# A decoder layer on one core: mixing buffers, four MLP down steps, and the final norm laid out differently

## The chip, the core and the metric

One NeuronCore of a Trainium2 chip runs the whole layer. Its engines are TensorE (PE in the profile: matmuls; PEld is its weight load), VectorE (DVE), ScalarE (ACT), GpSimd (POOL) and SyncE (SP), which issues the DMAs in order. Data live in SBUF (128 partitions), products are summed in PSUM (eight banks of 128x512 float32). The metric is the device time of one execution in microseconds; less is better. TensorE's clock has two levels, 1.2 and 2.4 GHz; the profile shows the granted clock as a fraction of the upper one.

## The reference, cut to what matters

With 1024 tokens and a model width of 1024 the layer computes

```python
u = rms_norm(x, norm_mix_g);  proj = u @ w_in
attn  = dilated_attention(rope(q), rope(k), v)       # 8 heads of 64, three window patterns
mlstm = sigmoid(mo) * rms(mlstm_chunkwise(q, k, v, gates))   # 4 heads of 128
h = x + concat(attn, mlstm) @ w_out
h = h + relu(rms_norm(h, norm_mlp_g) @ w_up) ** 2 @ w_down   # inner width 4096
h = h + sigmoid(rms_norm(h, norm_ple_g) @ w_ple_gate) * (p @ w_ple)
out = rms_norm(h, final_norm_g)
```

in float32. A reduced precision is not close enough, so every operand of a large product is split into a high and a low float32r part, and a product is three matmuls.

## The kernel before

All activations are held transposed: channels on partitions, tokens along the row, in KT = 8 blocks k of 128 channels and NCH = 2 halves c of CH = 512 tokens. `split` makes the two parts of an operand: a cast on ScalarE (L92) for the high part, a subtraction on VectorE (L93) for the low one. `mm3` issues wh·xh, wh·xl and wl·xh (L101 to L103).

**Order.** The program is written stage by stage, and a scheduler with planned costs of its own puts each engine's instructions, and SyncE's DMAs, into one fixed order, in which an engine works whatever the true times are. A tile of a pool waits until the tile that lay on its bytes before is no longer read; where one pool follows another this holds tile by tile.

**Mixing.** The projections and four pairs of attention heads work in a pool mp; when it is closed, the four mLSTM heads work in pools sp and cp on the same bytes. Attention results go to DRAM (mixd, L435), the values to vd (L446), mLSTM results to mixmd (L648). `head(h)` loads q and k as r, then qw (L547), the values vr (L567), and the decay weights w (L590). TensorE's transposes kt give kw, and `upd` (L576) updates the state with vr and kw. Beside the heads run the projections mvp of later heads. `load_pair` (L538) loads the mixed results `in` again and splits them into mixa (attention) and mixm (mLSTM), the operands of the out projection. `in` shares the tag "stage", four buffers, with other short-lived tiles, the t of the first out projection among them.

**First out projection.** `out_first(k)` sums four of the eight contributions: for each k and half, a tile t is loaded from xT (L663), the product o of twelve matmuls is added to it (L664), and it is stored to hd (L665). The rest of the out projection comes later.

**MLP.** MLP up runs 16 blocks f, each a scheme of seven products in place of eight. Its results zz and zt are stored to DRAM (zd, L891 and L898). MLP down has seven products D_OPS of eight steps g; a step is 24 matmuls d. For each step y (from zd) and wd are loaded raw, in a pool rawp, and split in a pool of two pairs (hl2) or in one of a single pair (hl1), in turn: every third step takes hl1. These pools lie on the bytes of the pools of MLP up: rawp and hl2 on the first ones, hl1 on the last, zu1, which holds the last block's result until it is stored. Only the first two steps are split into pairs of the general pool that MLP up has freed (`first`). After them come the additions to h (L1083).

**Gated embedding and final norm.** Four blocks o of 256 channels: seven products pg each (`embed`), the last block in two pieces of 256 tokens of each half. `gate` makes h of a channel block and token range: multiplication, tanh, two more on VectorE (L1133 to L1136), then h squared on ScalarE (L1140) and the running sum of squares fin, printed as state (L1144). `final_cols` sums the squares over channels with 128x1 matmuls cs (L1173), makes ra (L1178, VectorE) and rb, the reciprocal root (L1179, GpSimd). `final` spreads rb to rows with transposes bp (L130), copies them (L1187), and multiplies each of eight channel blocks by gain and row: on VectorE in one step (L1193), or on ScalarE and GpSimd (L1195, L1196). outT is stored channels first (L1199), and transposed on the host.

## Time and profile before

| | us |
|---|---|
| median of 3 runs | 1385.82 (1381.39 to 1387.63) |
| the profiled execution | 1385.74 |
| its span | 1383.9 |
| TensorE busy | 1330.2 (96%) |
| VectorE busy | 1021.7 (74%) |
| ScalarE busy | 655.6 (47%) |
| GpSimd busy | 58.0 (4%) |
| mean granted clock of TensorE | 0.982 |

All times in the trace count from the span's start. MLP down starts at 964.5, and the last product of the embedding ends at 1365.8. A row of a timeline with a count groups like instructions that follow each other; the name after the arrow is what is read.

### The profile page before, as it was taken

The page shows a single profiled execution, that of the slowest core. Times are in us where ns is not written, and L with a number is a line of the kernel's source. Part 1 is how long each engine was busy: PE and PEld are TensorE (multiplying, and loading weights), DVE is VectorE, ACT ScalarE, POOL GpSimd, SP SyncE. Part 2 cuts the span into 40 slices and gives each one's busy share as a digit, 9 for nine tenths or more (in the row PEclk, how much of TensorE's full clock was granted, in tenths as well). Part 3 has the DMA queues.
Part 4 walks back from the last instruction along what each step waited for, and adds up shares of the span by engine and source line. Part 5 has one row for each costly group of instructions (what it writes and reads, how often), then busy time and mean ns, then how long its engine had stood idle before and what let it go on. Part 6 is the DMA issues. An engine that isn't in the chain of part 4 may idle for free. (4 is left out here: it accounts for less than half of the span.)

```text
span 1383.9 us, 18363 instructions
## 1 busy us (share of the span) xinstructions
PE 1330.2 (96%) x6795; PEld 1120.7 (81%) x6795; DVE 1021.7 (74%) x1774; ACT 655.6 (47%) x1039; POOL 58.0 (4%) x55
## 2 busy tenths in 40 slices
PE   8999999999979998899999999999899999999995
PEld 6988888988859887788887888888788888888884
DVE  7797579599758885599666676667457875778895
ACT  7465545644446442258443334435234333565553
POOL 1100000000000000000000000000000210001002
PEclk9999999999999999999999999999999999999997
DMA  6111012123226347555154344446879773671323
GB/s 233 48 50 35 24 52 68 59 78 97 76 60 209 119 167 243 172 183 212 55 219 151 154 169 166 156 155 256 282 223 333 295 272 111 208 248 62 107 91 122
DMA packets 79018, 208.26 MB, mean 150 GB/s; under 512 B 7536, under 2 KB 19728, under 8 KB 74320
## 3 DMA queue, kind: packets, MB, share of 16 engines
q1 hardware_dynamic: 78928, 207.09, 43.6%
q8 instruction: 53, 0.87, 0.3%
q14 instruction: 37, 0.30, 0.1%
HBM read 146.74 MB, written 60.32 MB: 150 GB/s over the span
## 5 line engine op out<-in xcount | busy, mean ns | idle before, releaser
L102 PE MATMUL u<-x,wuh 128*128 128x512 f32 x448 | 177.0, 395 | 0.0
L101 PE MATMUL u<-x,wuh 128*128 128x512 f32 x448 | 174.7, 395 | 0.0
L103 PE MATMUL u<-x,wul 128*128 128x512 f32 x448 | 171.9, 395 | 1.0 <-DVE wul L93 1.0
L101 PE MATMUL d<-yh,wdh 128*128 128x512 f32 x432 | 166.0, 393 | 4.1 <-ACT wdh L92 3.7
L102 PE MATMUL d<-yl,wdh 128*128 128x512 f32 x432 | 168.7, 392 | 0.0
L103 PE MATMUL d<-yh,wdl 128*128 128x512 f32 x432 | 168.1, 391 | 0.0
L93 DVE TENSOR_TENSOR wul<-wu_r,wuh 128x768 fp32r<-128x768 f32 (+1 forms) x64 | 69.6, 1087 | 65.2 <-ACT wuh L92 65.2
L103 PEld LDWEIGHTS u<-x,wul 128*128 128x128 f32 x448 | 84.3, 188 | 21.1 <-DVE wul L93 1.4
L102 PEld LDWEIGHTS u<-x,wuh 128*128 128x128 f32 x448 | 84.4, 188 | 20.1 <-DVE x L93 0.4
L101 PEld LDWEIGHTS u<-x,wuh 128*128 128x128 f32 x448 | 84.3, 188 | 19.7
L101 PEld LDWEIGHTS d<-yh,wdh 128*128 128x128 f32 x432 | 81.7, 190 | 21.9 <-ACT wdh L92 4.2
L102 PEld LDWEIGHTS d<-yl,wdh 128*128 128x128 f32 x432 | 81.8, 189 | 17.2
L103 PEld LDWEIGHTS d<-yh,wdl 128*128 128x128 f32 x432 | 81.5, 189 | 16.9
L909 ACT COPY tmp<-u 128x512 f32<-128x512 f32 x48 | 28.1, 588 | 109.1 <-PE u L103 109.0
L92 ACT CAST wuh<-wu_r 128x768 fp32r<-128x768 f32 (+1 forms) x64 | 59.1, 943 | 43.2 <-PE u L102 22.2
L92 ACT CAST wdh<-wd_r 128x1024 fp32r<-128x1024 f32 x30 | 31.6, 1053 | 81.1 <-PE d L102 77.7
L93 DVE TENSOR_TENSOR wdl<-wd_r,wdh 128x1024 fp32r<-128x1024 f32 x30 | 36.6, 1220 | 43.8 <-ACT wdh L92 43.8
L410 ACT ACTIVATE pr<-pr,mn 128x128 f32<-128x128 f32 (+3 forms) x64 | 49.5, 774 | 41.0 <-PE av L413 23.4
L93 DVE TENSOR_TENSOR yl<-y_r,yh 128x1024 fp32r<-128x1024 f32 x54 | 65.6, 1216 | 0.0
L405 DVE CUSTOM_DVE_ANT_0 pr<-s,biasS 128x512 f32<-128x512 f32 (+2 forms) x96 | 51.0, 551 | 12.3 <-PE tp L420 7.2
L92 ACT CAST yh<-y_r 128x1024 fp32r<-128x1024 f32 x54 | 56.5, 1047 | 7.1 <-DMA y_r<-zd 7.1
L93 DVE TENSOR_TENSOR pl<-tp,ph 128x512 fp32r<-128x512 f32 (+1 forms) x80 | 49.7, 631 | 10.7 <-ACT ph L92 6.3
(393 smaller groups left out, 3410.4 us busy)
## 6 DMA issues: line engine op xcount, KB each, us to landing
wd_r<-wdown SPq DMA_DIRECT2D x72, 512.0 KB
y_r<-zd SPq DMA_DIRECT2D x56, 512.0 KB
wu_r<-wup SPq DMA_DIRECT2D x32, 512.0 KB
zd<-zz SPq DMA_DIRECT2D x16, 1024.0 KB
zd<-zt SPq DMA_DIRECT2D x16, 1024.0 KB
wm_r<-wmqk SPq DMA_DIRECT2D x8, 512.0 KB
wo_r<-wout SPq DMA_DIRECT2D x16, 256.0 KB
hs<-h SPq DMA_DIRECT2D x8, 512.0 KB
```

The lines of the kernel that those rows point to most:

```text
L92: S.copy(hi, src)
L93: V.tensor_tensor(lo, src, hi.bitcast(F32), op=ALU.subtract)
L101: PE.matmul(ps, wh, xh, start=start, stop=False, skip_group_check=more)
L102: PE.matmul(ps, wh, xl, start=False, stop=False, skip_group_check=more)
L103: PE.matmul(ps, wl, xh, start=False, stop=stop, skip_group_check=more)
L405: V.tensor_tensor_reduce(pr[:, ks], s[:, :n], biasS[:, b0 + o:b0 + o + n], 1.0, -2 * LOW, op0=ALU.add, op1=ALU.min, accum_out=mn[:, o // C ...
L410: S.activation(pr[:, :nk], pr[:, :nk], AF.Exp, scale=-1.0, bias=mn[:, :1], accum_out=den)
L909: S.copy(tmp[key], ps)
```

## The change

It has three parts.

*Mixing.* cosS and sinS are allocated ahead of KL in mp, which moves other tiles of that pool. In `head`, vr is loaded, and its ones are set, first, ahead of r and qw. `load_pair` gets four buffers of its own for `in`, in cp.

*MLP down.* Two more pairs for y and two for wd (`ahead`) are taken from the general pool before MLP up is closed, so the first four steps of product b11 lie there. The pairs for sw are taken when they are first written.

*Final norm.* h of a block and range is multiplied by its gain on ScalarE once its square is taken. The squares of k = 6 and k = 7 stay apart from fin, so that a column sum has three sources. The 64 blocks of 128x128 of h are transposed by TensorE (`turned`) into fixed PSUM banks, so that tokens lie on partitions, and rb becomes a factor for each partition: `result` multiplies 128x512 at a time from PSUM on ScalarE or VectorE, and stores outN, tokens first. No rows are spread, and the host transposes nothing.

```diff
+    cosS = mp.tile([P, T], F32, name="cosS", bufs=1)
+    sinS = mp.tile([P, T], F32, name="sinS", bufs=1)
     KL = [[mp.tile([P, T], F32R, name=f"kl{i}{a}", bufs=1) for a in range(2)] for i in range(2)]
...
     S.mul(ghalf, col[:, C_MG:C_MG + MH], 0.5)
-    cosS = mp.tile([P, T], F32, name="cosS", bufs=1)
-    sinS = mp.tile([P, T], F32, name="sinS", bufs=1)
     biasS = mp.tile([P, T], F32, name="biasS", bufs=1)
...
             sl = slice(c * CH, (c + 1) * CH)
-            r = stage("in")[:, :CH]
+            r = cp.tile([P, CH], F32, name="in", bufs=4)
             nc.sync.dma_start(r, src[:, sl])
...
     def head(h, qk=(None, None)):
+        vr = cp.tile([P, NB, P + 1], F32, name="vr", bufs=1)
+        nc.sync.dma_start(vr[:, :, :P], vd[h // 2, :, :, (h % 2) * P:(h % 2 + 1) * P])
+        V.memset(vr[:, :, P:], 1.0)
         r = raw(qkd[h]) if qk[0] is None else qk[0]
...
         vv = (unit("mv"), unit("mv"))
-        vr = cp.tile([P, NB, P + 1], F32, name="vr", bufs=1)
-        nc.sync.dma_start(vr[:, :, :P], vd[h // 2, :, :, (h % 2) * P:(h % 2 + 1) * P])
-        V.memset(vr[:, :, P:], 1.0)
         split([v.rearrange("p (b c) -> p b c", c=P) for v in vv], vr[:, :, :P])
...
                 if fresh:
-                    bank[b] = acc_tile(name)[:, :width]
+                    bank[b] = (banks[b] if banks else acc_tile(name))[:, :width]
                 for i in range(n):
...
         first = [[split(pair(n), r) for n, r in zip(("y", "wd"), raws)] for raws in first]
+        ahead = [[pair(n) for n in ("y", "wd")] for _ in range(2)]
         up_scope.close()
...
         def parts(name, tag, src):
+            if ahead and tag == "y":
+                return split(ahead[0][0], src)
+            if ahead:
+                return split(ahead.pop(0)[1], src)
             pool = hl1 if made[tag] % 3 == 2 else hl2
...
         A11, A12, A21, A22 = range(4)
-        sp4 = [pair("s", F32) for _ in range(NG // 2)]
-        sw = [sp4[g // 2][g % 2] for g in range(NG)]
+        sw = []
         def weights(key, g):
...
                 a, b = wraw(g, A21), wraw(g, A22)
+                if g % 2 == 0:
+                    sw.extend(pair("s", F32))
                 V.tensor_tensor(sw[g], a, b, op=ALU.subtract)
...
                 S.activation(fin[:, sl], h[k][:, sl], AF.Square)
+                S.mul(h[k][:, sl], h[k][:, sl], col[:, C_GFIN:C_GFIN + 1])
                 return
             S.activation(ga, h[k][:, sl], AF.Square)
-            if k == KT - 1:
-                last[sl.start] = ga
+            if k >= KT - 2:
+                last[k, sl.start] = ga
             else:
                 V.tensor_tensor(fin[:, sl], fin[:, sl], ga, op=ALU.add)
-        def embed(o, off=0, n=CH, hooks={}):
+            S.mul(h[k][:, sl], h[k][:, sl], col[:, C_GFIN + k:C_GFIN + k + 1])
+        def embed(o, off=0, n=CH, hooks={}, banks=None):
             tmp = {}
...
                     f()
-            products(wblocks[o], X, ev, "pg", off=off, width=n)
+            products(wblocks[o], X, ev, "pg", off=off, width=n, banks=banks)
+        FINAL = [slice(c * CH + a, c * CH + a + L) for a in (0, L) for c in (1, 0)]
         cols_of = {}
-        def final_cols(i):
+        def sums(i, *which):
             sl = FINAL[i]
-            nt = (sl.stop - sl.start) // P
-            cs = acc_tile("cs3")
-            for j in range(nt):
-                for src in (fin[:, sl], last[sl.start]):
-                    PE.matmul(cs[:, j:j + 1], src[:, j * P:(j + 1) * P], ones, start=src is not last[sl.start],
-                              stop=src is last[sl.start])
-            a = zp.tile([P, nt], F32, name="ra3", tag="ra")
-            b = cols_of[i] = zp.tile([P, nt], F32, name="rb3", tag="rb")
-            at = slice(sl.start // P, sl.stop // P)
-            V.scalar_tensor_tensor(a, cs[:, :nt], 1.0 / D, seps[:, at], op0=ALU.mult, op1=ALU.add)
-            G.tensor_tensor(b, a, mhalf[:, :nt], op=ALU.pow)
-        def final(i):
-            sl = FINAL[i]
-            n = sl.stop - sl.start
-            bp = acc_tile("bp3")
-            bcast_rows(bp, cols_of[i], n // P)
-            rows = small("rows")[:, :n]
-            S.copy(rows, bp[:, :n])
-            outs = wcp.tile([P, 8, L], F32, name="out", tag="wc")
-            for k in range(KT):
-                o = outs[:, k]
-                gain = col[:, C_GFIN + k:C_GFIN + k + 1]
-                if k in ON_V[i]:
-                    V.scalar_tensor_tensor(o, h[k][:, sl], gain, bp[:, :n], op0=ALU.mult, op1=ALU.mult)
-                else:
-                    S.mul(o, h[k][:, sl], gain)
-                    G.tensor_tensor(o, o, rows, op=ALU.mult)
-                if k + 1 in TO[i]:
-                    k0 = max(t for t in (0,) + TO[i] if t <= k)
-                    nc.sync.dma_start(outT[k0:k + 1, :, sl].rearrange("k p t -> p k t"), outs[:, k0:k + 1])
-        ON_V = ((0, 1, 3, 4, 6), (0, 1, 3, 4, 6, 7), (0, 1, 3, 4, 6), (0, 2, 3, 5, 6, 7))
-        TO = ((4, 8), (4, 8), (4, 8), (2, 4, 6, 8))
-        FINAL = [slice(c * CH + a, c * CH + a + L) for a in (0, L) for c in (1, 0)]
+            n = L // P
+            to = [banks[3 if i == 3 and j else 0][:, CH // 2 + 2 * i + j:CH // 2 + 2 * i + j + 1] for j in range(n)]
+            for j, src in ([(j, src) for src in which for j in range(n)] if i == 3 else
+                           [(j, src) for j in range(n) for src in which]):
+                at = fin[:, sl] if src == "fin" else last[src, sl.start]
+                PE.matmul(to[j], at[:, j * P:(j + 1) * P], ones, start=src == "fin", stop=src == KT - 1)
+            if KT - 1 in which:
+                a = zp.tile([P, n], F32, name="ra3", tag="ra")
+                b = cols_of[i] = zp.tile([P, n], F32, name="rb3", tag="rb")
+                t0 = sl.start // P
+                for at in ((slice(0, 1), slice(1, 2)) if i == 3 else (slice(0, 2),)):
+                    src = banks[3 if at.start else 0][:, CH // 2 + 2 * i + at.start:CH // 2 + 2 * i + at.stop]
+                    V.scalar_tensor_tensor(a[:, at], src, 1.0 / D, seps[:, t0 + at.start:t0 + at.stop],
+                                           op0=ALU.mult, op1=ALU.add)
+                G.tensor_tensor(b, a, mhalf[:, :n], op=ALU.pow)
+        def turned(i, ks, js=(0, 1)):
+            for k in ks:
+                for j in js:
+                    t0 = FINAL[i].start + j * P
+                    PE.transpose(banks[TB[i][2 * j + k // 4]][:, k % 4 * P:(k % 4 + 1) * P], h[k][:, t0:t0 + P], ident)
+        def result(i):
+            outs = wcp.tile([P, 8, L], F32, name="out", tag="wc").rearrange("p a b -> p (a b)")
+            tb = FINAL[i].start // P
+            for j in range(2):
+                for q in range(2):
+                    o = outs[:, j * D + q * CH:j * D + (q + 1) * CH]
+                    src = banks[TB[i][2 * j + q]]
+                    r = cols_of[i][:, j:j + 1]
+                    if (q if i >= 2 else 2 * j + q == 1):
+                        V.tensor_scalar(o, src, r, None, op0=ALU.mult)
+                    else:
+                        S.activation(o, src, AF.Copy, scale=r)
+                    nc.sync.dma_start(outN[tb + j, :, q * CH:(q + 1) * CH], o)
+        TB = ((2, 5, 6, 7), (2, 5, 6, 7), (1, 4, 5, 2), (6, 7, 1, 4))
         fetch(0)
...
         fetch_emb(NO - 1)
-        embed(NO - 1, 0, L)
-        embed(NO - 1, L, L, hooks={"b11": [lambda: final_cols(0)], "b22": [lambda: final(0)],
-                                   "t3": [lambda: final_cols(1)], "t4": [lambda: final_cols(2)]})
-        final_cols(3)
-        for i in range(1, 4):
-            final(i)
+        banks = [acc_tile("fin") for _ in range(8)]
+        embed(NO - 1, 0, L, banks=dict(x=banks[0], z=banks[1], y=banks[2]))
+        A, B = KT - 2, KT - 1
+        first_k = range(KT - 2)
+        hooks = dict(t2=[lambda: sums(0, "fin", A, B)], b22=[lambda: turned(0, range(KT))],
+                     t3=[lambda: result(0), lambda: sums(1, "fin", A, B)],
+                     b21=[lambda: turned(1, range(KT))])
+        embed(NO - 1, L, L, hooks=hooks, banks=dict(x=banks[3], z=banks[4], y=banks[0]))
+        result(1)
+        sums(2, "fin", A, B)
+        turned(2, range(KT))
+        turned(3, first_k, (0,))
+        sums(3, "fin", A)
+        sums(3, B)
+        turned(3, (A, B), (0,))
+        result(2)
+        turned(3, range(KT), (1,))
+        result(3)
```

On SyncE, the load of vr of the first head now stands between the last store of mixd and the load of qw, where it stood behind qw; on TensorE 27 matmuls mvp of the row just ahead of the first upd stand before it, where there were 33. In SyncE's queue in the first out projection (in is a mixed result, t takes x, h is the same block read again for the next norm, wo_r a weight), before:

```order
L538 DMA in_5943<-mixmd_82 128x512
L665 DMA hd_85<-t_5929 128x512
L81 DMA wo_r_6082<-wout 128x512
L538 DMA in_5947<-mixmd_82 128x512
L852 DMA h_6295<-hd_85 128x1024
L663 DMA t_5970<-xT 128x512
L663 DMA t_5987<-xT 128x512
L663 DMA t_6010<-xT 128x512
L81 DMA wo_r_6118<-wout 128x512
L663 DMA t_6027<-xT 128x512
```

After, the place of the same t loads:

```order
L664 DMA t_5912<-xT 128x512
L649 DMA mixmd_82<-sgl_5292 128x512
L664 DMA t_5929<-xT 128x512
L853 DMA h_6213<-hd_85 128x1024
L664 DMA t_5970<-xT 128x512
L625 DMA sgl_5781<-sgd_89 128x512
L666 DMA hd_85<-t_5889 128x512
L81 DMA wo_r_6031<-wout 128x512
L664 DMA t_5987<-xT 128x512
L853 DMA h_6253<-hd_85 128x1024
L666 DMA hd_85<-t_5912 128x512
```

The t loads of xT no longer follow the four loads of in from mixmd; they stand between the stores of the t tiles.

On ScalarE, where MLP up passes into MLP down (y and wd are operands, the casts make their high parts; before, 9035 and 9041 belong to step two, 9071 and 9077 to three, 9153 to five, 9191 to six, 9109 and 9115 to four), before:

```order
L92 CAST yh_9035<-y_r_9033 128x1024
L92 CAST wdh_9041<-wd_r_9039 128x1024
L92 CAST yh_9071<-y_r_9069 128x1024
L92 CAST wdh_9077<-wd_r_9075 128x1024
L890 ACTIVATE zz_8801<-zz_8801 128x2048
L92 CAST wdh_9153<-wd_r_9151 128x1024
L92 CAST yh_9147<-y_r_9145 128x1024
L92 CAST wdh_9191<-wd_r_9189 128x1024
L92 CAST yh_9185<-y_r_9183 128x1024
L92 CAST yh_9109<-y_r_9107 128x1024
L92 CAST wdh_9115<-wd_r_9113 128x1024
```

After, from the last cast of step three on (8956 is step three, 9101 and 9107 four, 9145 five, 9221 seven, 9177 and 9183 six):

```order
L92 CAST wd_8956<-wd_r_9069 128x1024
L891 ACTIVATE zz_8801<-zz_8801 128x2048
L92 CAST yh_9101<-y_r_9099 128x1024
L92 CAST wdh_9107<-wd_r_9105 128x1024
L92 CAST wdh_9145<-wd_r_9143 128x1024
L92 CAST yh_9139<-y_r_9137 128x1024
L92 CAST wdh_9221<-wd_r_9219 128x1024
L92 CAST yh_9215<-y_r_9213 128x1024
L92 CAST yh_9177<-y_r_9175 128x1024
L92 CAST wdh_9183<-wd_r_9181 128x1024
```

Step four's casts stand directly behind zz now; step six's stand behind those of step seven.

On TensorE, at the end of the program, the rows from the last column sums on (fin_11840 and the next are PSUM banks, h the blocks k, ga the squares of k = 6 and 7), after:

```order
L1187 MATMUL fin_11843<-ones_72,ga_12144 128x1
L1202 MATMUL fin_11847<-ident_69,h_8977 128x128
L1187 MATMUL fin_11840<-ones_72,state_8979 128x1
L1187 MATMUL fin_11840<-ones_72,ga_12108 128x1
L1187 MATMUL fin_11840<-ones_72,ga_12144 128x1
L1202 MATMUL fin_11847<-ident_69,h_8978 128x128
L1202 MATMUL fin_11841<-ident_69,h_8971 128x128
L1202 MATMUL fin_11841<-ident_69,h_8972 128x128
L1202 MATMUL fin_11841<-ident_69,h_8973 128x128
L1202 MATMUL fin_11841<-ident_69,h_8974 128x128
L1202 MATMUL fin_11844<-ident_69,h_8975 128x128
```

Before, the last rows were column sums cs3 and the transposes bp that spread rb:

```order
L1173 MATMUL cs3_12122<-ones_72,state_8979 128x1
L130 MATMUL bp3_12131<-ident_69,rb3_12071 128x128 x2
L1173 MATMUL cs3_12122<-ones_72,ga_12107 128x1
L1173 MATMUL cs3_12122<-ones_72,state_8979 128x1
L1173 MATMUL cs3_12122<-ones_72,ga_12107 128x1
L130 MATMUL bp3_12149<-ident_69,rb3_12119 128x128 x2
L130 MATMUL bp3_12168<-ident_69,rb3_12128 128x128 x2
```

The last ten transposes, eight of them of one token block into two banks, stand behind the last column sums; three more like the last row end the program.

## Rows read from the trace of the kernel before

**Rows 1.** The page, part 1: engines' busy us, share of the span, instructions.
```profile
PE 1330.2 (96%) x6795; PEld 1120.7 (81%) x6795; DVE 1021.7 (74%) x1774; ACT 655.6 (47%) x1039; POOL 58.0 (4%) x55
```
**Rows 2.** TensorE's waits by cause: total us, times, longest us.
```profile
PE o L101 <- DVE t L664: 5.1, 1, 5.1
...
PE upd L576 <- DVE qw L549: 4.1, 1, 4.1
PE d L101 <- ACT wdh L92: 3.7, 1, 3.7
PE bp L130 <- POOL rb L1179: 3.3, 1, 3.3
...
PE cs L1173 <- DVE state L1144: 2.7, 2, 1.6
PE pg L101 <- DVE ga L1157: 2.3, 2, 1.8
```
**Rows 3.** Busy time by window: engines, TensorE's granted clock, DMA share, GB/s.
```profile
555.01:559.01 4.00, 4.00 (x9) 3.17 (x10) 2.03 (x9) 0.00 (x0) 1.01 (x1) 0.50 0.70 263
990.30:996.00 5.70, 5.70 (x14) 4.45 (x15) 1.69 (x2) 0.00 (x0) 1.35 (x3) 0.51 0.82 293
1300.00:1320.00 20.00, 20.00 (x88) 16.13 (x87) 18.53 (x30) 10.34 (x17) 0.00 (x0) 1.00 0.28 83
1365.70:1384.00 18.30, 5.19 (x23) 4.32 (x22) 9.91 (x27) 4.89 (x13) 6.27 (x9) 0.50 0.56 188
```
**Rows 4.** SyncE's timeline at the first mLSTM head: start us, us, what, count.
```profile
406.46 1.80 SPq L547 DMA_DIRECT2D qw<-arow  x1
408.32 0.60 SPq L567 DMA_DIRECT2D vr<-vd  x1
```
**Rows 5.** ScalarE's timeline there; in brackets the idle time before and its releaser.
```profile
413.59 1.05 ACT L92 CAST mv<-vr 128x1024 fp32r<-128x1024 f32 x1 [0.88 <-DMA vr<-vd]
```
**Rows 6.** Chain of waits, last block: start us, us, what.
```profile
1353.74 1.05 PE cs L1173 x8
...
1364.59 0.13 PE pg L101
1364.71 0.21 PE pg L102
```
**Rows 7.** SyncE's timeline in the first out projection.
```profile
548.15 0.32 SPq L538 DMA_DIRECT2D in<-mixmd  x1
...
549.00 1.37 SPq L663 DMA_DIRECT2D t<-xT  x3
...
561.05 0.38 SPq L538 DMA_DIRECT2D in<-mixmd  x1
```
**Rows 8.** ScalarE's timeline at the start of MLP down.
```profile
986.28 1.04 ACT L92 CAST wdh<-wd_r 128x1024 fp32r<-128x1024 f32 x1 [3.44 <-PE d L102]
...
989.13 1.04 ACT L92 CAST wdh<-wd_r 128x1024 fp32r<-128x1024 f32 x1
```
**Rows 9.** TensorE's timeline there, the first product of MLP down.
```profile
964.51 0.40 PE L101 MATMUL d<-y,wd 128*128 128x512 f32 x1
```
**Rows 10.** SyncE's timeline there, the last store of MLP up's result.
```profile
975.68 0.37 SPq L898 DMA_DIRECT2D zd<-zt  x1
```
**Rows 11.** TensorE's timeline in attention: transposes of 128x128.
```profile
377.61 1.06 PE L420 MATMUL tp<-ident,pr 128*128 128x128 f32 x8
...
395.05 1.71 PE L420 MATMUL tp<-ident,pr 128*128 128x128 f32 x7 [2.31 <-DVE pl L93]
```
**Rows 12.** VectorE's timeline in the final norm.
```profile
1369.28 0.16 DVE L1178 SCALAR_TENSOR_TENSOR ra<-cs,seps 128x2 f32<-128x2 f32 x1 [0.50 <-PE cs L1173]
...
1376.60 2.44 DVE L1193 SCALAR_TENSOR_TENSOR out<-h,col,bp 128x256 f32<-128x256 f32 x6 [1.50 <-DMA outT<-out]
```
**Rows 13.** GpSimd's timeline there.
```profile
1374.39 0.70 POOL L1179 TENSOR_TENSOR rb<-ra,mhalf 128x2 f32<-128x2 f32 x1
```
**Rows 14.** The page, part 5: ScalarE's 128x512 copy, busy us, mean ns.
```profile
L909 ACT COPY tmp<-u 128x512 f32<-128x512 f32 x48 | 28.1, 588 | 109.1 <-PE u L103 109.0
```

More of the change, by code (lines that the diff above doesn't have):

```diff
@@ L46, in layer_kernel @@
 def layer_kernel(ctx, tc, xT, wqk, wv, wvg, wmv, wmqk, wmo, wout, wup, wdown, wpg, wple, pT,
-                 cols, cosT, sinT, biasT, identT, maskT, lastT, belowT, outT):
+                 cols, cosT, sinT, biasT, identT, maskT, lastT, belowT, outN):
     nc = tc.nc
@@ L764, in load_blocks, with products @@
             return wa, wb
-        def products(w, x, evac, name, own=(), off=0, width=CH):
+        def products(w, x, evac, name, own=(), off=0, width=CH, banks=None):
             bank = {}
@@ L1299 @@
             for n, v in arrays.items()]
-    args.append(nc.dram_tensor("outT", (KT, P, T), F32, kind="ExternalOutput").ap())
+    args.append(nc.dram_tensor("outN", (NB, P, D), F32, kind="ExternalOutput").ap())
     with tile.TileContext(nc, schedule_with_timeline_sim=True) as tc:
@@ L1303 @@
     r = _run(nc, [arrays], core_ids=[0])
-    out = np.asarray(r.results[0]["outT"]).reshape(D, T)
-    return np.ascontiguousarray(out.T).reshape(1, T, D)
+    return np.asarray(r.results[0]["outN"]).reshape(1, T, D)
```

## The prediction

> **What bounds the kernel now.** The profiled execution took 1385.74 us: a span of 1383.9 us and 1.84 us around it. The median of the runs, 1385.82 us, is the same within their spread, so the sum is made from 1385.74. The page's busy table comes first: TensorE is busy for 1330.2 us of the span [rows 1], so a change that leaves its products alone can return at most some 54 us. Next, the table of what TensorE waits for, summed by cause [rows 2]. The waits are few and long: 5.1 us for t in the first out projection, 4.1 us at an mLSTM state update, 3.7 us at an early MLP down step, and in the last block and the final norm 3.3, 2.7 and 2.3 us. Then the clock beside them: after the first and the third of these waits the granted clock is 0.50 and 0.51 for 4.00 and 5.70 us, though TensorE is fully busy, and from the last product to the end it is 0.50 again [rows 3]. 1.0 is the 2.4 GHz level and 0.5 the 1.2 GHz level. So a long wait costs itself and about half of the stretch of slow products behind it. The change touches just these places; elsewhere TensorE is the bound (20.00 of 20 us in a stretch of the embedding blocks [rows 3]).
>
> **First mLSTM head (vr).** On SyncE the load of qw is issued at 406.46 for 1.80 us and that of vr at 408.32 for 0.60 us [rows 4]. ScalarE's cast of vr starts at 413.59 after a wait for vr's DMA [rows 5]: landing takes 413.6 − 408.9 = 4.7 us from the end of the issue. The update reads vr and kw, not qw. TensorE's 4.1 us wait for it [rows 2] ends with vr's landing at about 413.6, so it began at about 409.5, although the table names qw's multiply. In the new order vr's load stands where qw's stood: issued from 406.46 to 407.06, landed at 411.8 if the latency holds, 1.8 us earlier. But six 128x256 products that stood ahead of the update now stand behind it; at 0.13 us each (the row before the clock fell [rows 6]) they save 0.8 us ahead and cost it behind. The wait becomes 411.8 − 408.7 = 3.1 us: gain 1.0 us. Landing has been seen only once here, so I allow 1 us either way: bounds 0 and 2.0. qw's own load slips by 0.6 us; its first reader comes after the update, so it hides.
>
> **First out projection (t, in).** TensorE's longest wait is for t = x + o. The loads of t are issued as a group of three from 549.00, directly behind the in load of 548.15 [rows 7]. Both use one tag of four buffers before, so a load of x waits until a buffer with a mixed result has been read, and SyncE, which takes its issues in order, holds everything behind. With an in tag of its own, the t loads can run ahead of the projection. In the new issue order the t loads stand before the mixm loads that they used to follow. A t buffer then comes back after four t steps of twelve 128x512 products, 4 x 12 x 0.23 = 11 us, against a round trip of load, addition and store of some 7 to 9 us (two DMAs of near 4 us, as vr's, and 0.7 us), so no wait is left. That returns 5.1 us, and the stretch at half clock, 4.00 us at 0.50 [rows 3], returns 2.0: 7.1 together. New waits can come: the first products of this projection now stand ahead of the last head's scores, and the mixa casts and subtractions that feed them are planned just in time; the loads of the second half of mixa still wait for four buffers to be read. The stretch had waits of up to 5.1 us, and the short ones in the table elsewhere are 1 to 2 us, so I charge 1.5 us, between nothing and 4: gain 5.6, bounds 3 and 7.1. The reordering also shuffles products where TensorE was full; I price that at 0, with 3 us either way.
>
> **Four down steps ahead** (steps counted from zero). Before, ScalarE casts the weight of a later step, in a buffer that a previous step must free, ahead of those of step four: that cast starts at 986.28 after waiting for TensorE's own products, and step four's weight is cast at 989.13 [rows 8]. TensorE waits 3.7 us for it. With four steps in buffers that MLP up has freed, steps two and three don't take the two pairs of the pool, step four and five do, without waiting for any product. That removes 3.7 us, and half of the 5.70 us at 0.51, 2.8 [rows 3]. What is late next: the same trap one cycle on. The cast for step seven waits for the end of step four and stands ahead of that for step six, which alone uses the single third pair. Steps take 24 products; a 128x512 product takes 0.227 us at full clock (88 in 20.00 us [rows 3]), so a step takes 5.45. The down stage starts at 964.5 [rows 9], so step four ends at 991.8. Four casts of 1.05 us [rows 8] follow, to 996.0, and step six is due at 964.5 + 6 x 5.45 = 997.2. The subtraction for its low part ends at about 997.4. I charge 0.3 us: gain 6.2. That pair lies on the buffer whose contents the zt store of 975.68 must have read [rows 10]; the store is now issued some 3.5 us later, behind one load, and would be done by about 988, against 993.8 when it is needed. Bounds: 3 if step six waits 3 us with its own clock loss, 6.5 if nothing waits.
>
> **Final norm.** Removed are the broadcasts, 42 small multiplications on three engines and their order behind each other; added are 64 transposes of 128x128 and 16 evacuations of 128x512. Eight transposes take 1.06 us, 0.13 each, in attention; seven take 1.71 us, 0.245 each, right behind a wait [rows 11]. Before the last product, 38 of them (4.9 us) and four more sums than before (eight records of half a sum each take 1.05 us, 0.26 a sum [rows 6], 1.0 us) are put in, and two broadcasts go (0.3). They fill holes: TensorE waited 2.7 us for the sums' inputs and 2.3 us for the gates there [rows 2]. So the last product ends 5.6 − 5.0 = 0.6 us later, at 1366.4. Behind it, before: 18.1 us, namely 3.5 to the reduced sums at 1369.28, then VectorE's multiplications of three slices, with the last ra only behind five of these, rb on GpSimd behind three more (0.70 us at 1374.39 [rows 13]), the last six from 1376.60 to 1379.04 [rows 12], and 4.9 to the end. After: 3.5 to the sums, 0.2 and 0.7 for ra and rb, four evacuations of 0.59 on ScalarE (the price of its 128x512 copy [rows 14]; as many on VectorE beside them), 2.4, 1.3 in which the last eight transposes wait for a bank and run, and 4.9: 13.0. That is 5.1 less; minus 0.6 is 4.5. The clock is 0.50 in the tail before [rows 3], so I add 0.115 for each of the ten transposes that stand behind the sums, 1.1 us, and take a gain of 3.4. Bounds: 5 with all hidden; 0 if the holes don't take the inserted work and two waits of 2 us remain. The fourteen multiplications by the gain on ScalarE, about 0.6 us each, lie where it is busy for 10.34 of 20 us [rows 3] and VectorE for 18.53; they are free, and VectorE's running sum of squares gets one term shorter.
>
> The sum: 1.0 + 5.6 + 6.2 + 3.4 = 16.2 us, so 1385.74 − 16.2 = 1369.5.
>
> **A rule weighed.** Eight adjacent transposes at 0.13 each run without any sign of a slower clock. The Trainium skill ("TensorE: Matmul & The Clock Gate", Part 4: PE-mode transpose) says that in one kernel's context a transpose took about 275 ns and that this mode doesn't count as busy for the clock in the way that products do. By 275 ns, an estimate from that page, the 38 transposes would take 10.5 us rather than 4.9, and the norm would lose about 2 us instead of gaining 3.4.
>
> **The rivals.** *Half clock in the last block.* As a mechanism of this kernel: if the clock falls once transposes are mixed into the last half block, the 38 cost 0.245 each (4.4 us more), some 48 of its 128x256 products 0.21 rather than 0.13 [rows 6], 3.8 more, and the sums 1.0 more: the norm gives −5.8 and the time is 1385.74 − 12.8 + 5.8 = 1378.7. The page's sentence on the clock speaks for it; the eight at 1.06 us speak against. 7 in 100.
>
> *The waits only move.* The update waits as long as before (0), new waits in the out projection leave 3, step six waits (3), the tail gives 1.5: 7.5 us, 1378.2. For it: three of the four terms have a next wait within 1 to 2 us of its due time. Against: the margins are all worked out from durations that hardly vary. 20 in 100, spread over 1375 to 1381.
>
> *Everything lands.* 2.0 + 7.1 + 6.5 + 5 = 20.6, and up to 3 from the shuffled stretch: 1362 to 1365. 10 in 100.
>
> *Slower: SyncE is held at the in loads.* These loads were spread wide before: after 548.15 the next was issued at 561.05, 12.9 us later [rows 7]. The second four mixa loads now stand in SyncE's queue ahead of the last head's gates and weights and of the first x loads, and wait until the first four buffers are read. If SyncE is held for 12.9 us twice (mixa's second half, then mixm), with 2 us of slack each time, TensorE stands for 22 us; the out projection's 5.6 is lost as well, so the time is 1385.74 − 10.6 + 22 = 1397. It decides against the change from about 11 us of holding. Against it: the four buffers are read by VectorE in 0.7 us steps, and the planner has put work in between. 4 in 100.
>
> **How the numbers follow.** The forecast, 1366 to 1374, gets 59 in 100. About 0.5%, 6.9 us, is what a measurement of this kernel can tell from no change, so faster means below 1378.9. Faster: 59 + 10 + 12 (of the moved waits) + 3 (half the half-clock case) = 84, less 4 for what the table of waits doesn't show: 80. Same: 15. Slower: 5. The range takes in the bounds up to the moved waits, 1362 to 1379.
>
> **What would show it.** In the profile after, the table of waits should have no line for t and none above 1 us at the down steps; the update's line should stand at about 3 us. The granted clock should be above 0.9 in the 20 us slices about the out projection and the down stage's start. From the last product to the end should be 13 to 14 us, and the transposes should take 0.13 us each up to there. I am wrong if a wait of over 2 us stands at the down stage's sixth or seventh step, at the first product of the out projection or at the last head's scores, or if transposes take 0.25 us before the last product.

## The result, and the profile after

The changed kernel takes 1372.4 us (median of 4, 1370.91 to 1373.37) against 1386.72 for the kernel before on the same chip: ratio 0.9899, 95% interval 0.9878 to 0.9919. The forecast was 1369.5, the range 1362 to 1379. The profiled execution took 1370.91 us with a span of 1369.1.

The page's busy line answers [rows 1]:

```profile
PE 1336.8 (98%) x6867; PEld 1127.8 (82%) x6867; DVE 1017.0 (74%) x1755; ACT 666.3 (49%) x1055; POOL 53.2 (4%) x45
```

TensorE is busy 6.6 us longer (the 64 transposes are the added work) and idle 32.3 us instead of 53.7. Its table of waits, the lines that answer [rows 2] and the new ones (total us, times, longest us):

```profile
PE upd L577 <- DMA vr<-vd: 2.0, 1, 2.0
...
PE cs L124 <- DVE sgl L647: 0.7, 1, 0.7
...
PE sc L101 <- DVE state L581: 0.5, 1, 0.5
...
PE o L101 <- ACT mixa L92: 0.3, 1, 0.3
PE fin L1202 <- ACT out L1215: 0.3, 1, 0.3
PE o L101 <- DVE c L641: 0.2, 1, 0.2
```

The lines for t, for wdh, for rb, and those for the sums and gates of the last block are gone; upd is left at 2.0. New are short ones: the column sums cs behind sgl, o behind mixa and behind c, and fin behind out; the scores sc waited 0.3 us before. The windows that answer [rows 3] (time, then busy us by engine, granted clock of TensorE, DMA share, GB/s); the first lies behind the new wait of cs:

```profile
461.90:465.90 4.00, 4.00 (x17) 3.35 (x17) 2.75 (x10) 0.60 (x1) 0.00 (x0) 0.65 0.82 246
...
510.00:530.00 20.00, 19.24 (x103) 16.45 (x102) 15.66 (x38) 7.82 (x18) 1.01 (x1) 0.83 0.94 320
...
990.30:996.00 5.70, 5.70 (x26) 4.72 (x26) 4.85 (x5) 2.76 (x3) 1.04 (x1) 1.00 0.91 281
...
1355.60:1369.10 13.50, 6.20 (x51) 5.61 (x48) 5.12 (x12) 4.92 (x10) 1.39 (x2) 0.69 0.48 176
```

The clock is 1.00 where MLP down had 0.51 before, but 0.65 at 461.9, behind sums where it was 1.00 before, and 0.83 in 20 us of the first out projection, where the prediction wanted more than 0.9. ScalarE at the start of MLP down answers [rows 8]:

```profile
987.16 1.05 ACT L92 CAST wdh<-wd_r 128x1024 fp32r<-128x1024 f32 x1 [16.16 <-PE d L102]
...
990.02 1.04 ACT L92 CAST wdh<-wd_r 128x1024 fp32r<-128x1024 f32 x1
```

The casts that stand behind a wait for TensorE (16.16 us, end of step four) are those of step seven and, last, of step six: it ends at 991.1, and step six is due at 992.7 (the stage starts at 960.0, six steps of 5.45). No wait follows. TensorE behind the last product answers [rows 11]:

```profile
1355.46 1.91 PE L1202 MATMUL fin<-ident,h 128*128 128x128 f32 x16
1357.20 0.28 PE L1187 MATMUL fin<-ones,state 128*128 128x1 f32 x2
...
1360.44 1.63 PE L1202 MATMUL fin<-ident,h 128*128 128x128 f32 x8 [0.27 <-ACT out L1215]
```

Sixteen transposes in 1.91 us at full clock, and the last eight in 1.63, 0.2 each, at half clock.

Where the time went, from TensorE's rows (us, gains taken before rounding; "mixing" counts from the first value product mvp that waits for v, near 406, to the start of the last product of the first out projection; the last two rows are parted by the start of the last product):

| | before | after | gain |
|---|---|---|---|
| mixing | 171.1 | 166.5 | 4.7 |
| MLP down | 313.3 | 306.8 | 6.4 |
| last down product to last product | 87.6 | 88.5 | −0.9 |
| last product to end of span | 18.6 | 13.8 | 4.8 |

These make 15.0 us; the spans differ by 14.8, since the stretches between lost 0.2.

### The profile page after: what moved, and what is told of

Same layout as the page of the kernel before. It is cut to its first block, busy times and chain, and to the rows that moved or that the text cites. A ratio compares the mean times of both kernels' runs of the same rounds, so it can differ in the third digit from the quotient of the medians.

```text
span 1369.1 us, 18476 instructions
## 1 busy us (share of the span) xinstructions
PE 1336.8 (98%) x6867; PEld 1127.8 (82%) x6867; DVE 1017.0 (74%) x1755; ACT 666.3 (49%) x1055; POOL 53.2 (4%) x45
## 4 chain that ended last, share of the span: by engine, by line
PE 87%; DVE 5%; DMA 4%; ACT 2%; issue 1%; SPq 1%; DVEq 0%; POOLq 0%; ACTq 0%
PE u L102 8%; PE u L103 8%; PE u L101 8%; PE d L101 7%; PE d L102 7%; PE d L103 7%; PE tp L421 2%; PE o L102 2%; PE o L101 2%; PE o L103 2%; PE m L103 2%; PE m L101 2%; PE m L102 2%; PE pg L101 1%; PE pg L103 1%; PE pg L102 1%
## 5 line engine op out<-in xcount | busy, mean ns | idle before, releaser
L101 PE MATMUL u<-x,wuh 128*128 128x512 f32 x448 | 174.3, 394 | 0.0
L102 PE MATMUL d<-yl,wdh 128*128 128x512 f32 x416 | 161.4, 389 | 0.0
L103 PE MATMUL d<-yh,wdl 128*128 128x512 f32 x416 | 161.2, 389 | 0.0
L101 PE MATMUL d<-yh,wdh 128*128 128x512 f32 x416 | 158.6, 390 | 0.7 <-DVE h L1090 0.7
L101 PEld LDWEIGHTS d<-yh,wdh 128*128 128x128 f32 x416 | 78.0, 188 | 17.3 <-issue 1.1
L103 PEld LDWEIGHTS d<-yh,wdl 128*128 128x128 f32 x416 | 78.1, 188 | 16.3
L102 PEld LDWEIGHTS d<-yl,wdh 128*128 128x128 f32 x416 | 78.1, 188 | 16.0
L92 ACT CAST wdh<-s 128x1024 fp32r<-128x1024 f32 x24 | 25.2, 1050 | 66.0 <-PE d L102 59.1
```

Of the source, the lines that this page charges most:

```text
L92: S.copy(hi, src)
L101: PE.matmul(ps, wh, xh, start=start, stop=False, skip_group_check=more)
L102: PE.matmul(ps, wh, xl, start=False, stop=False, skip_group_check=more)
L103: PE.matmul(ps, wl, xh, start=False, stop=stop, skip_group_check=more)
```

## Experiments

All ratios are against the kernel before, run on the same chip. "Mixing" and the other stretches are those of the table.

### One part taken back at a time

**The old MLP down** (u1):

```diff
-        ahead = [[pair(n) for n in ("y", "wd")] for _ in range(2)]
...
-        sw = []
+        sp4 = [pair("s", F32) for _ in range(NG // 2)]
+        sw = [sp4[g // 2][g % 2] for g in range(NG)]
```

> The changed kernel with the old allocation of MLP down alone (two steps ahead, the sw pairs taken at once). Theory (a wait of TensorE for step four's casts, and half clock behind it, was what this part removed): the wait d <- wdh of about 3.7 us returns at step four, the granted clock falls to about 0.5 for some 5.7 us behind it, and the time is 6.4 us above the changed kernel's: span about 1375.5, ratio to the kernel before about 0.9945. Rival (the down stage gains from its other pools or its DMA order, not from this wait): the wait is there but the stage from its first product to its last takes less than 311 us; then the time rises by under 4 us.

Measured: 1379.84 us, ratio 0.9950 (0.9933 to 0.9967). The wait is back at its old size:

```profile
PE d L101 <- ACT wdh L92: 3.7, 1, 3.7
```

MLP down takes 313.5 us, and the granted clock from 990.3 to 996.0 is 0.50. In the eleven profiles with the new allocation (the changed kernel and the other experiments that keep it whole) it takes 305.9 to 307.5. So this part gives 6.0 to 7.6 us in every profile; its rival, a stage of under 311 us, did not come. The medians differ by 7.4 us. The spans of the two profiles differ by 11.3, of which MLP down makes 6.7 and mixing, 170.5 us here, 4.1.

**The old final norm** (u2), the change's hunks from `gate` to the end taken back:

```diff
-            S.mul(h[k][:, sl], h[k][:, sl], col[:, C_GFIN + k:C_GFIN + k + 1])
...
-        result(3)
+        final_cols(3)
+        for i in range(1, 4):
+            final(i)
```

> The changed kernel with the old final norm alone. Theory (the norm gained 4.5 us behind the last product and lost 0.7 us ahead of it): from the last product to the end takes 18 us again, the wait bp <- rb of 3.3 us is back, and the time is 3.8 us above the changed kernel's: span about 1372.9, ratio about 0.9927. Rival (the gain behind the last product was paid for by the gains and squares moved ahead, so that undoing it gives back most): a rise of under 2 us.

Measured: 1378.04 us, ratio 0.9936 (0.9913 to 0.9958), span 1377.3. From the last product to the end 18.3 us, with the wait bp <- rb of 3.3 us. So the norm's part is 4.5 us behind the last product, as expected. The median rose by 5.6 us where 3.8 were expected. In the profiles the span rose by 8.1, of which mixing, whose code is that of the changed kernel, makes 4.9 (171.4 instead of 166.5). Mixing is not steady, which neither theory said.

**The old mixing** (u3), with cosS and sinS in their old place too:

```diff
-            r = cp.tile([P, CH], F32, name="in", bufs=4)
+            r = stage("in")[:, :CH]
...
         vv = (unit("mv"), unit("mv"))
+        vr = cp.tile([P, NB, P + 1], F32, name="vr", bufs=1)
+        nc.sync.dma_start(vr[:, :, :P], vd[h // 2, :, :, (h % 2) * P:(h % 2 + 1) * P])
```

> The changed kernel with the old mixing pools and the old place of vr's load. Theory (mixing gained 4.4 us up to the last product of the first out projection): the waits o <- t of 5.1 and upd of 4.1 us return, with half clock behind both, and the last product of the first out projection ends at about 576.7 instead of 572.3; the time is 3.5 to 4.5 us above the changed kernel's: span about 1373, ratio about 0.993. Rival (mixing's part gave nothing that lasts, since SyncE, the scores or the second half of the out projection took it back): a rise of under 2 us.

Measured: 1375.05 us, ratio 0.9914 (0.9897 to 0.9930). Mixing takes 174.3 us, with both old waits, the longer one at 7.7 us:

```profile
PE o L101 <- DVE t L665: 7.7, 1, 7.7
...
PE upd L577 <- DMA vr<-vd: 4.6, 1, 4.6
```

The median lies 2.65 us above the changed kernel's: less than expected, more than the rival. The two ratios differ by 0.0015 and their intervals overlap, so this rise isn't clear of the noise.

**The changed kernel once more** (r1).

> The changed kernel itself, once more, to see what varies in it from one execution to the next. In two kernels with the same mixing stage the first out projection ended at 576.5 and 576.8 instead of 572.3, with waits for vr of 3.2 instead of 2.0 us and for t (behind c on VectorE) of 0.6 and 2.9 instead of 0.2. Theory (these landings vary by a microsecond or two and each late one brings half clock): the projection ends anywhere from 572 to 577 and the time is 1371 to 1377. Rival (the mixing stage is steady, and the others differ because of their own stages): it ends at 572.3 within 0.5, time 1371 to 1373.

Measured: 1371.02 us (1370.06 to 1371.34), ratio 0.9901 (0.9886 to 0.9915). Mixing 169.1: out projection to 573.9, upd waits 3.1, t behind c 1.2. Over all six profiles with this mixing stage (after, r1, u1, u2, x1, x2) mixing takes 166.5 to 171.4 us, mean 169.2, and upd waits 2.0 to 3.2. The two with the old one take 171.1 and 174.3, mean 172.7. So mixing's gain is 3.5 us, with some 2 us either way.

**Early vr or own buffers alone.** u4 has only the first piece of u3's diff:

> The changed kernel in which only the loaded mixed results use the shared tag again; vr's load stays first. Theory (the shared buffers held the loads of x): a wait o <- t of 3 us or more is back in the first out projection, and the last product of that projection ends 2 to 4 us later than the changed kernel's 572.3; span about 1372. Rival (the order of the queue, not the buffers, held them, and the early vr gave the new order): no wait for t over 1 us, and the projection ends within 1 us of 572.3.

u5 has only the second piece:

> The changed kernel in which only vr's load stands in its old place, behind r and qw; the mixed results keep their own buffers. Theory (vr first is what mixing gained by, and own buffers only trade the wait for t for other waits): the wait at upd is 4.1 us or more again, there is no wait for t's load, but waits of 0.5 us or more at the mixa casts, at t behind c, or at the scores; the first out projection ends at 577 to 580, the time is 3 to 5 us above the changed kernel's. Rival (own buffers are worth the 5 us of the wait for t): the projection ends by 574.

u4 measured 1370.87 us, ratio 0.9884 (0.9866 to 0.9902), mixing 167.7, with the wait for t back, as expected; the out projection ends at 573.4, 1.1 us later and not 2 to 4:

```profile
PE o L101 <- DVE t L665: 4.4, 1, 4.4
...
PE upd L577 <- DMA vr<-vd: 0.9, 1, 0.9
```

u5 measured 1365.88 us, ratio 0.9858 (0.9841 to 0.9874), mixing 163.9. Its waits from the first update to MLP up:

```profile
PE upd L577 <- DVE qw L550: 4.5, 1, 4.5
...
PE o L101 <- ACT woh L92: 1.2, 1, 1.2
...
PE bp L130 <- DVE h L661: 0.8, 1, 0.8
...
PE num L102 <- DVE mpl L93: 0.5, 1, 0.5
...
PE o L103 <- DVE wol L93: 0.4, 1, 0.4
...
PE kt L562 <- DVE mn L406: 0.2, 1, 0.2
```

So the shared buffers did hold the loads of x, as the prediction said, and my expectation for u5 was wrong: own buffers are not a mere trade. With vr in its old place, mixing takes 163.9 us with own buffers and 172.7 without; with vr first, 169.2 with and 167.7 without. The gains of the two edits don't add: own buffers alone gain more than both, and vr first alone gains about as much as both (u4's interval overlaps with those of the changed kernel). u4 and u5 keep the new place of cosS and sinS, the kernel before and u3 the old one; what that move does by itself was not tried, so some of the 8.8 us between 163.9 and 172.7 may be its own.

### What the two together bring in

One of the new waits is that of o behind c. Its chain is plainest in u2, where it is longest. TensorE, VectorE, ScalarE and SyncE there:

```profile
559.22 0.40 PE L103 MATMUL o<-mixa,wo_l 128*128 128x512 f32 x1
562.56 0.77 PE L101 MATMUL o<-mixa,wo_h 128*128 128x512 f32 x1 [2.94 <-DVE c L641]
```

```profile
558.02 0.69 DVE L93 TENSOR_TENSOR mixm<-in,mixm 128x512 fp32r<-128x512 f32 x1 [6.42 <-ACT mixm L92]
560.45 0.69 DVE L93 TENSOR_TENSOR mixm<-in,mixm 128x512 fp32r<-128x512 f32 x1 [1.74 <-ACT mixm L92]
...
561.73 0.69 DVE L665 TENSOR_TENSOR t<-t,o 128x512 f32<-128x512 f32 x1
```

```profile
557.37 0.62 ACT L92 CAST mixm<-in 128x512 fp32r<-128x512 f32 x1 [7.71 <-DMA in<-mixmd]
559.80 0.62 ACT L92 CAST mixm<-in 128x512 fp32r<-128x512 f32 x1 [1.81 <-DMA in<-mixmd]
```

```profile
553.43 0.33 SPq L664 DMA_DIRECT2D t<-xT  x1
553.86 0.86 SPq L539 DMA_DIRECT2D in<-mixmd  x2
```

SyncE issues the last two loads of mixed results at 553.86, behind a load of x that waits until its buffer has been stored. ScalarE's casts wait for them (7.71 us of idle time), VectorE's subtractions for the casts, and the addition of t at 561.73 stands behind these in VectorE's order, though TensorE's last product before its stop ended at 559.6. TensorE's next product starts when this addition has ended, so I read the 2.94 us as a wait for the PSUM bank that it frees; the table names c, which stands next and which the product doesn't read. In the other five profiles of this mixing stage the same wait is 0.2 to 1.2 us. In the changed kernel's first profile SyncE issues the two loads at 551.66, 2.2 us earlier, and they land about as fast; what held SyncE back in u2 was not followed.

This wait is the smaller part of what the two edits cost together. Take TensorE's waits in mixing and half of its busy time at half clock as lost: in all profiles but x3's the rest of mixing is then 155 to 157 us, so these two make up the differences. Cut by time (us lost):

| mixing as in | up to 430 (first head) | 430 to 505 | 505 to the end |
|---|---|---|---|
| before, u3 (neither edit) | 6.8, 7.0 | 0, 0 | 8.8, 11.5 |
| u4 (vr first) | 3.4 | 0 | 8.7 |
| u5 (own buffers) | 6.9 | 0.5 | 1.7 |
| the changed kernel's six profiles (both) | 3.7 to 5.8 | 2.5 to 4.8 | 3.2 to 6.6 |

Only with both edits does the middle lose more than 0.5 us: 0.8 to 1.4 us in waits, the 0.7 ahead of the third group of column sums among them, and 1.7 to 3.4 through half clock behind the third and, in four of the six profiles, the fourth group.

**Six buffers** (v1, v2, v3) change the order of t's additions:

```diff
-        return sp.tile([P, CH + 3], F32, name=name, tag="stage")
+        return sp.tile([P, CH + 3], F32, name=name, tag="stage", bufs=6)
```

v1 has this diff with `in` in the shared tag and vr first; v2 the same with vr in its old place; v3 has own buffers, six instead of four, and vr first.

> The changed kernel with the loaded mixed results in the shared tag again, but six buffers in that tag instead of four and vr's load first. Theory (it is the number of buffers that held the loads of x, and the planner then puts the additions of t ahead of the last mixed results on VectorE, so that no new wait comes): no wait for t over 1 us, none behind c; the first out projection ends at 568 to 570, time 1366 to 1369. Rival (any way of giving the loads room makes new waits elsewhere in the stage): it ends at 572 or later, time 1371 or more.

> Six buffers in the shared tag for the loaded mixed results, and vr's load in its old place; down and norm as changed. With the other runs this fills the table of vr's place against the buffers. Theory (the buffers end the wait for t in any order; vr's place is worth 2 to 3 us at the first update but also sets the planner's order): no wait for t over 1 us, a wait of 4 us at upd; from the end of attention to the last product of the first out projection 163 to 166 us, against 162.2 with vr first and six buffers; time 1367 to 1370. Rival (the old place of vr is better in itself, since the kernel with own buffers and the old place was the faster one): that stretch takes 161 us or less, time 1362 to 1365.

> The changed kernel with six instead of four own buffers for the loaded mixed results. The planner then puts the additions of t ahead of the last subtractions of mixm on VectorE. Theory (in the changed kernel the additions of t stood behind mixm's subtractions, which waited for a late load): no wait of TensorE for c or t over 0.3 us in the first out projection, which ends 1 to 4 us earlier after the end of attention than the changed kernel's; time 1366 to 1371. Rival (that wait is only one of several small ones that this way of loading brings): as many waits at the sums and scores as before, time 1371 or more.

| | vr | `in` | upd waits | mixing | time | ratio |
|---|---|---|---|---|---|---|
| v1 | first | shared, 6 | 0.9 | 162.1 | 1366.76 | 0.9873 (0.9858 to 0.9887) |
| v2 | old | shared, 6 | 4.5 | 163.4 | 1366.44 | 0.9875 (0.9856 to 0.9893) |
| v3 | first | own, 6 | 1.0 | 163.3 | 1369.29 | 0.9890 (0.9873 to 0.9907) |

All three lose the wait of t behind c (v2 keeps 0.5 us for t), and what was expected of them came, but for v2's time, 0.6 us below its range. With six buffers the planner puts more additions of t ahead of the last subtractions of mixm. v3 differs from the changed kernel in this number alone; but the whole stage is ordered anew with it. Of the 5.9 us by which its mixing is shorter than the mean of the six, it loses 1.3 less in the first head, 2.3 less from 430 to 505 and 1.2 less behind 505, so the order of t's additions can be the direct cause of the last alone. v3's time isn't clear of the changed kernel's. The medians of u5, v1 and v2 lie 4 to 6.5 us under the changed kernel's, 3.3 to 6 by the ratios; only u5's interval lies wholly under the changed kernel's. Which of the three is best isn't settled. A place for vr outside the bytes of attention, so that it could be loaded earlier, was not tried.

### The clock

In the changed kernel's mixing the clock falls where no long wait stands. v1 shows it (TensorE's timeline; the nearest wait, 0.36 us, ends 3.5 us ahead of the sums):

```profile
509.84 0.29 PE L103 MATMUL sc<-mq,mk 128*128 128x256 f32 x1
...
510.53 0.95 PE L124 MATMUL cs<-ones,sq 128*128 128x1 f32 x8
511.33 1.03 PE L124 MATMUL cs<-ones,w 128*128 128x1 f32 x8
...
513.01 0.42 PE L102 MATMUL sc<-mq,mk 128*128 128x256 f32 x1
...
514.93 0.63 PE L102 MATMUL o<-mixa,wo_h 128*128 128x512 f32 x1
```

Behind sixteen column sums of 128x1, which TensorE ran without a gap, a score product of 128x256 takes 0.42 instead of 0.29 us and a 128x512 product 0.63, where u2's row has 0.40: half clock for some 3.5 us. In r1 the nearest wait lies 16 us ahead of the fourth group, and the 4 us behind it show the same:

```profile
478.54:482.54 4.00, 4.00 (x19) 3.52 (x18) 2.86 (x9) 1.20 (x3) 0.00 (x0) 0.58 0.57 206
```

Most groups of sixteen leave the clock at 1.00. To test the sums, each of the eight groups was done twice (x3):

```diff
-        col_sum(fb, sq, 0, n=nt)
-        for i in range(2):
-            col_sum(fb, w2[:, i], nt + 2 * i, n=2)
+        for _ in range(2):
+            col_sum(fb, sq, 0, n=nt)
+            for i in range(2):
+                col_sum(fb, w2[:, i], nt + 2 * i, n=2)
```

> The changed kernel in which each of the eight groups of sixteen column sums of 128x1 in the mLSTM heads is done twice over, so that 32 follow each other; the second pass writes the same sums. In the runs so far the granted clock fell to half right behind one to three of these eight groups, in some places with no wait of TensorE near. Theory (these narrow sums, though the page counts them as busy time, are what lets the clock fall): with twice as many in a row the granted clock is below 0.8 in the 4 us behind five or more of the eight groups. Rival (the clock falls for waits of TensorE only): behind no more than the two or three groups that also have a wait; each pass costs only its own 1.75 us.

Measured: 1392.91 us, ratio 1.0065 (1.0046 to 1.0083). TensorE's timeline at the first group, and windows of 4 us behind the first, sixth, seventh and last group:

```profile
429.97 0.28 PE L103 MATMUL mvp<-mv_h,x 128*128 128x256 f32 x1
...
430.89 1.03 PE L124 MATMUL cs<-ones,w 128*128 128x1 f32 x8
...
432.68 1.73 PE L124 MATMUL cs<-ones,w 128*128 128x1 f32 x8
...
435.38 0.41 PE L103 MATMUL num<-mph,mv 128*128 128x128 f32 x1
```

```profile
434.40:438.40 4.00, 4.00 (x21) 4.00 (x21) 2.85 (x8) 1.51 (x4) 0.00 (x0) 0.50 0.70 225
...
523.60:527.60 4.00, 4.00 (x20) 3.33 (x20) 3.53 (x9) 1.09 (x2) 0.00 (x0) 1.00 0.60 184
560.60:564.60 4.00, 4.00 (x13) 3.42 (x14) 1.72 (x8) 0.60 (x1) 1.01 (x1) 0.50 0.76 262
578.00:582.00 4.00, 4.00 (x19) 3.25 (x19) 2.32 (x9) 0.62 (x1) 1.01 (x1) 1.00 0.88 250
```

The last eight sums of the first group already take 1.73 us instead of 1.03, and the 4.00 us behind them, in which TensorE is fully busy, have a clock of 0.50. Behind the second to fifth group it is 0.57, 0.50, 0.50 and 0.57; only behind the sixth and the last it stays 1.00. Of the six that fall, two have a wait of TensorE near: 0.80 us just ahead of the seventh, and 0.78 us 1.4 us ahead of the third. The other four have none. That is six of eight, where two or three fell with sixteen sums: the narrow sums let the clock fall, and a wait isn't needed. In the changed kernel a wait of 0.68 us stands ahead of the third group, and the clock fell there in all six profiles, while it stayed at 1.00 behind the third group in u3, u4, u5, v1, v2 and v3 and in the kernel before, where no such wait stands.

**Transposes doubled** (x1): every transpose of the final norm issued twice:

```diff
                 for j in js:
                     t0 = FINAL[i].start + j * P
+                    for _ in range(2):
-                    PE.transpose(banks[...
+                        PE.transpose(banks[...
```

> The changed kernel in which each of the final norm's 64 transposes is done twice, to price them: the second one writes the same result. Theory (a transpose costs 0.11 us of TensorE at full clock and transposing does not let the clock fall): from the last down product to the last product 4.2 us more than the 88.5 of the changed kernel, the granted clock stays 1.00 up to the last column sums, and the time behind the last product grows by 1 to 2.5 us. Rival (transposes do not count as work for the clock): the granted clock falls in the last block, and the block grows by more than 8 us.

Measured: 1376.58 us, ratio 0.9944 (0.9929 to 0.9958). The last block takes 91.6 us, 3.1 more (38 at 0.11 would be 4.2; some fill waits), and the tail 13.7, no more than before: of the two parts expected, the second did not come. The windows of the last block and the tail, and TensorE's longest row of transposes:

```profile
1340.00:1350.00 10.00, 10.00 (x89) 10.00 (x88) 6.36 (x17) 7.13 (x18) 0.70 (x1) 1.00 0.09 28
1350.00:1361.00 11.00, 11.00 (x100) 11.00 (x98) 6.63 (x16) 6.55 (x15) 0.98 (x1) 1.00 0.41 150
1361.00:1374.20 13.20, 8.46 (x77) 8.22 (x77) 4.33 (x10) 4.38 (x9) 1.47 (x2) 0.98 0.52 195
```

```profile
1361.85 4.13 PE L1203 MATMUL fin<-ident,h 128*128 128x128 f32 x36
```

The clock is 1.00 throughout the block, with twice as many transposes, and 0.98 in the tail, with 36 in a row. The page of the Trainium skill weighed in the prediction ("TensorE: Matmul & The Clock Gate", Part 4: PE-mode transpose) doesn't hold for these float32 transposes: 0.11 us each in a row, and no loss of clock. A single one lasts 0.31 us in the changed kernel's timeline (at 1359.13), near the 275 ns that the Trainium skill gives there, which is no price for many in a row. 1.6 us of the rise in the span is MLP down (307.5 against 305.9 in r1), which isn't touched.

**Three steps ahead instead of four** (x2):

```diff
-        ahead = [[pair(n) for n in ("y", "wd")] for _ in range(2)]
+        ahead = [[pair(n) for n in ("y", "wd")] for _ in range(1)]
```

> The changed kernel with three instead of four down steps in buffers freed by MLP up. Steps three and four take the two pairs of the pool, step five the single third pair; its casts stand behind those of step six, which wait for the end of step three. Theory (what counted was that no cast with a wait for TensorE stands ahead of a cast that is due at once): step three ends 21.8 us after the stage's start, four casts take 4.1 us, step five is due at 27.2, so no wait; the stage takes 306 to 307.5 us, the time is that of the changed kernel. Rival (each step ahead is worth its own buffers): a wait for wdh of over 1 us at step five, the stage takes 309 us or more.

Measured: 1373.57 us (1369.16 to 1376.32), ratio 0.9914 (0.9891 to 0.9938). There is no wait for wdh, MLP down takes 307.8 us, 0.3 above the expected span; 1.6 us of it is a wait for an addition of h, which is at most 1.4 in the others. So the fourth step's buffers aren't needed for the gain. That what counts is which casts stand behind one that waits for TensorE fits u1 and this run; no run changed the order of the casts alone.

## Why the prediction was right, and where not

The time lies inside the range and near the forecast: 14.3 us were gained where 16.2 were forecast. By its terms:

- **vr**: a wait of 3.1 us was worked out; the six profiles have 2.0 to 3.2. The mechanism is right: the table's line says vr now. The load landed faster than assumed, 3.8 to 4.1 us from the end of its issue to ScalarE's cast instead of 4.7, but in five of the six its issue took 1.4 to 1.8 us instead of 0.6. Half clock behind the wait shrank too, which wasn't counted: up to 430 us the stage lost 6.9 us with the old mixing and 4.7 with the new (means), a gain of 2.2 where 1.0 was forecast.
- **t and in**: forecast 5.6. The wait for t did go, with its half clock; u3 and u4 show it where the shared tag is back. Behind 505 us the loss fell from 10.2 to 4.4, a gain of 5.8, but from 430 to 505 a loss of 4.0 came that wasn't there before: 1.8 is left (mixing's 3.5 is the 2.2 and this 1.8, less 0.5 that the rest took more). The step that failed is the charge of 1.5 us for new waits. In the changed kernel's first profile they come to 1.6 us (cs 0.7, sc 0.5, mixa 0.3, c 0.2), in r1 to 3.0 with kt's 0.5, and I had given them no half clock, nor seen that column sums bring it. It costs 1.4 us behind the third group of sums (0.65 for 4 us) and about as much behind one or two later groups. I also priced the reordering at 0 with 3 us either way; u5 and v1 show that other orders of the same work take 5 to 7 us less.
- **Down steps**: forecast 6.2, measured 6.4, and u1 undoes 6.7. Step six had no wait at all; its casts were done 1.6 us ahead.
- **Final norm**: forecast 3.4, measured 3.8 (4.78 less 0.94), in u2 4.5 behind the last product. The last product came 0.9 us later, near the 0.6, but that is in part luck. The 2.7 us of waits for the sums' inputs that were to be filled don't all lie ahead of the last product; 1.6 of them lie behind it, in the kernel before:

```profile
1367.37 0.59 PE L1173 MATMUL cs<-ones,state 128*128 128x1 f32 x2 [1.59 <-DVE state L1144]
```

  The transposes, at 0.11 us instead of 0.13, made up for part of it. The 1.1 us for slow transposes was too much: only the last eight ran at half clock.
- **Rivals**: x1 speaks against half clock through transposing. SyncE was not held at the in loads for long: o waits 0.3 us for mixa. "The waits only move" is true in part of mixing and false of the down steps and the norm. So the total came out near the forecast because vr, the down steps and the norm gave a little more than forecast and t and in a good deal less.

## What to carry to other kernels

Before a part that frees a queue is priced, look at which instructions the planner then puts ahead of the freed ones on each engine, and which of them wait for a load: a wait that names one operation often belongs to the one queued before it. Two edits that each remove a wait can be worth less together, so try each alone. A new wait, even a short one, should be priced with the half clock that can follow it. Where a cast waits for TensorE, put what is due at once ahead of it in the order; here buffers for one more step were enough for that.

## What the runs showed of the hardware that I had not expected

TensorE's clock fell from 2.4 to 1.2 GHz behind some groups of sixteen 128x1 column sums with no wait near, and behind six of eight groups of 32, though the profile counts these 1.8 or 3.6 us as busy. In x1, 36 float32 transposes of 128x128 in a row, 4.13 us, did not bring it down. Of waits, 1.00 us in the kernel before left the clock at 1.00 (TensorE's timeline; it stays there until 552):

```profile
526.77 0.38 PE L101 MATMUL num<-mph,mv 128*128 128x256 f32 x1 [1.00 <-ACT mph L92]
```

0.68 us ahead of such sums brought half clock in six profiles of six.
